# Batched matmul on one core: longer weight runs with quarter-lane casts on two engines, and a store lag that grows

## Chip, cores, metric

One NeuronCore of a Trainium2 chip. The metric is the time of one execution in microseconds on the device. Engines are named as the profile names them: PE (TensorE), DVE (VectorE), ACT (ScalarE), SP (SyncE, which here issues every DMA). Sixteen DMA engines serve the core. PSUM is the memory that PE writes its results to. A lane is one of the 128 partitions that an instruction works on at a time.

## The reference

```python
x:      (8, 16, 256, 512) float32
weight: (8, 16, 512, 384) float32
out = np.matmul(x, weight)          # 128 products of 256x512 by 512x384
```

That is 67.1 MB of x, 100.7 MB of weights and 50.3 MB of results: 218.1 MB in all.

## The kernel before

Four of the 128 products make a group, 32 groups in all. Per group the kernel loads x (2 MB, runs of 16 KB: 8 rows of a partition) and the weights (two loads of 1.5 MB, runs of 12 KB), casts both to bf16, transposes x on PE, multiplies, copies the result out of PSUM and stores it (1.5 MB, runs of 12 KB). DVE casts the weights, ACT casts x and copies results out.

```python
G = 4; C = P // G; R = G * M // P; T = R // 2      # C = 32, R = 8, T = 4
D = 2; S = 2; HP = P // D                          # two products stacked in one weight load
XS, WS, OS = 2, 2 * G // D, 4                      # x, weight and output buffers
LAG = 4                                            # stores run four groups behind loads
...
def load(e, t, U, s):                              # on SP
    e.wait_ge(x_cast, ...)                         # x buffer free: x of group n-2 is cast
    e.dma_start(x_sb[s % XS][:], ...)
    for d in range(G // D):
        e.wait_ge(w_cast, ...)                     # weight buffer free: its casts are done
        e.dma_start(w_sb[slot][:], ...rearrange("(p k) n -> p k n", k=S * KO))
...
def prepare(e, t, U, s):                           # on DVE
    for d in range(G // D):
        e.wait_ge(w_in[slot], ...)
        for a in range(D):
            for h in range(S):                     # 8 casts of 64 lanes x 1536 per group
                e.tensor_copy(out=w_bf[...][h * HP : (h + 1) * HP], in_=w_sb[slot][...])
    for q in range(T):
        e.tensor_copy(out=x_t[...], in_=pt[...])   # transposed x out of PSUM
...
def step(t, U, s, more):                           # on ACT
    for q in range(T):
        copy_out(e, t, U, s, q)
        if q == 1 and more:
            cast_x(e, t, U, s + 1)                 # x of the next group
```

All DMAs go through one queue in program order. So a load that waits for its buffer also holds back what comes after it.

Of the kernel before, what the change touches and what calls it, by code (L numbers as in the profile page):

```python
# [11 lines left out]
def kernel(  # L12
# [7 lines left out]
    P = 128  # L20

    b1, b2, M, K = x.shape
    _, _, _, N = weight.shape
    B = b1 * b2
    KO = K // P

    x_rows = x.rearrange("b1 b2 m k -> (b1 b2 m) k")
    w_rows = weight.rearrange("b1 b2 k n -> (b1 b2 k) n")
    o_rows = out.rearrange("b1 b2 m n -> (b1 b2 m) n")

    fp32 = mybir.dt.float32
    bf16 = mybir.dt.bfloat16
# [2 lines left out]




    G = 4
    C = P // G  # L40
    R = G * M // P
    T = R // 2
    D = 2
    S = 2
    HP = P // D
    NG = B // G

    XS, WS, OS = 2, 2 * G // D, 4
    BS, TS, WBS = 1, 2, 2 * G
    PT, PO = 4, 2  # L50

    LAG = 4

    ctx.enter_context(tc.tile_critical(no_gpsimd_drain=True))  # L54

    def sbuf(name, shape, dtype, n):
        return [
            ctx.enter_context(nc.sbuf_tensor(f"{name}{s}", shape, dtype)) for s in range(n)
        ]
# [6 lines left out]
    def sems(name, n):  # L66
        return [tc.alloc_semaphore(f"{name}{s}") for s in range(n)]
# [2 lines left out]
    identity = sbuf("identity", [P, P], fp32, 1)[0]  # L70
    x_sb = sbuf("x_sb", [P, R, K], fp32, XS)

    x_bf = sbuf("x_bf", [P, R, S, HP, KO], bf16, BS)
    x_t = sbuf("x_t", [P, R, KO // 2, P, 2], bf16, TS)
    w_sb = sbuf("w_sb", [P, S * KO, N], fp32, WS)
    w_bf = sbuf("w_bf", [P, KO, N], bf16, WBS)
    out_sb = sbuf("out_sb", [P, R, N], fp32, OS)
    pt = psum("pt", [P, 2, KO // 2, P], fp32, PT)
    po = psum("po", [P, 2, 512], fp32, PO)
# [1 line left out]



    id_done, x_cast, w_cast, t_made, t_copied, p_made, o_copied = (
        sems(name, 1)[0]
        for name in (
            "id_done", "x_cast", "w_cast", "t_made", "t_copied", "p_made", "o_copied"
        )
    )
    x_in, w_in, o_out = sems("x_in", XS), sems("w_in", WS), sems("o_out", OS)  # L90


    BIAS = 8


    def load(e, t, U, s):
        n = t * U + s
        if not isinstance(n, int) or n >= XS:
            e.wait_ge(x_cast, n + (1 - XS))
        e.dma_start(  # L100
            x_sb[s % XS][:],
            x_rows[bass.ds(n * (G * M), G * M)].rearrange("(p r) k -> p r k", r=R),
        ).then_inc(x_in[s % XS], 16)
        for d in range(G // D):
            slot = (s * (G // D) + d) % WS
            if not isinstance(n, int) or n >= 2:
                e.wait_ge(w_cast, n * (G * S) + ((d + 1) * D * S - 2 * G * S))
            e.dma_start(  # L108
                w_sb[slot][:],
                w_rows[bass.ds(n * (G * K) + d * (D * K), D * K)].rearrange(  # L110
                    "(p k) n -> p k n", k=S * KO
                ),
            ).then_inc(w_in[slot], 16)

    def store(e, t, U, s, pieces=1):
        n = t * U + s
        dram = o_rows[bass.ds(n * (G * M), G * M)].rearrange("(p r) n -> p r n", r=R)
        for q in range(pieces):
            rows = slice(q * R // pieces, (q + 1) * R // pieces)
            e.wait_ge(o_copied, n * T + ((q + 1) * T // pieces + BIAS))  # L120
            e.dma_start(out=dram[:, rows], in_=out_sb[s % OS][:, rows]).then_inc(
                o_out[s % OS], 16
            )

    def cast_x(e, t, U, s):
        n = t * U + s
        e.wait_ge(x_in[s % XS], (t * (U // XS) + s // XS) * 16 + 16)
        e.wait_ge(t_made, n * T + ((1 - BS) * T + BIAS))
        for h in range(S):
            ins = e.copy(  # L130
                out=x_bf[s % BS][:, :, h],
                in_=x_sb[s % XS][:].rearrange("p r (q s c) -> p r s q c", s=S, c=KO)[
                    :, :, h
                ],
            )
        ins.then_inc(x_cast, 1)

    def prepare(e, t, U, s):
        n = t * U + s
        e.wait_ge(p_made, n * T + (BIAS - T))  # L140
        for d in range(G // D):
            slot = (s * (G // D) + d) % WS
            e.wait_ge(  # L143
                w_in[slot], (t * (U * G // D // WS) + s * G // D // WS) * 16 + 16
            )
            for a in range(D):
                for h in range(S):
                    e.tensor_copy(  # L148
                        out=w_bf[(s * G + d * D + a) % WBS][h * HP : (h + 1) * HP],
                        in_=w_sb[slot][a * HP : (a + 1) * HP, h * KO : (h + 1) * KO, :],  # L150
                    ).then_inc(w_cast, 1)
        for q in range(T):
            e.wait_ge(t_made, n * T + (q + 1 + BIAS))
            e.tensor_copy(  # L154
                out=x_t[s % TS][:, 2 * q : 2 * q + 2],
                in_=pt[(s * T + q) % PT][:].bitcast(bf16),
            ).then_inc(t_copied, 1)

    def multiply(e, t, U, s):
        n = t * U + s  # L160
        words = x_bf[s % BS][:].rearrange("p r s q c -> p r (s q c)").bitcast(fp32)
        e.wait_ge(x_cast, n + 1)
        for q in range(T):
            e.wait_ge(t_copied, n * T + (q + 1 - PT + BIAS))
            for rr in range(2):
                for h in range(KO // 2):
                    ins = e.transpose(  # L167
                        pt[(s * T + q) % PT][:, rr, h, :],
                        words[:, 2 * q + rr, h :: KO // 2],
                        identity[:],  # L170
                    )
            ins.then_inc(t_made, 1)
        e.wait_ge(w_cast, n * (G * S) + G * S)
        for q in range(T):
            e.wait_ge(t_copied, n * T + (q + 1 + BIAS))
            e.wait_ge(o_copied, n * T + (q + 1 - PO + BIAS))
            for rr in range(2):
                for ko in range(KO):
                    for i in range(G):
                        mine = slice(i * C, (i + 1) * C)  # L180
                        ins = e.matmul(  # L181
                            po[(s * T + q) % PO][mine, rr, :N],
                            x_t[s % TS][:, 2 * q + rr, ko // 2, mine, ko % 2],
                            w_bf[(s * G + i) % WBS][:, ko, :],
                            start=(ko == 0),
                            stop=(ko == KO - 1),
                        )
            ins.then_inc(p_made, 1)

    def copy_out(e, t, U, s, q):  # L190
        n = t * U + s
        if q == 0:
            e.wait_ge(o_out[s % OS], (t * (U // OS) + s // OS) * 16 + 16)
        e.wait_ge(p_made, n * T + (q + 1 + BIAS))
        e.copy(  # L195
            out=out_sb[s % OS][:, 2 * q : 2 * q + 2, :],
            in_=po[(s * T + q) % PO][:, :, :N],
        ).then_inc(o_copied, 1)
# [6 lines left out]

    def on_sync(e):
        U = OS
        for n in range(LAG):
            load(e, 0, NG, n)
        rounds = (NG - LAG) // U  # L210
        with e.Fori(0, rounds) as t:
            for s in range(U):
                load(e, t, U, LAG + s)
                store(e, t, U, s)
        for n in range(rounds * U, NG):
            if n + LAG < NG:
                load(e, 0, NG, n + LAG)
            store(e, 0, NG, n, T if n == NG - 1 else 1)
        for s in range(OS):
            e.wait_ge(o_out[s], 16 + 16 * (NG // OS + (T - 1 if s == (NG - 1) % OS else 0)))  # L220

    def on_vector(e):
        U = 2
        e.sem_inc(t_copied, BIAS)
        with e.Fori(0, NG // U) as t:  # L225
            for s in range(U):
                prepare(e, t, U, s)

    def on_tensor(e):
        U = 2  # L230
# [7 lines left out]
    def on_scalar(e):  # L238
        U = OS
        e.sem_inc(o_copied, BIAS)  # L240
        for s in range(OS):
            e.sem_inc(o_out[s], 16)

        def step(t, U, s, more):
            for q in range(T):
                copy_out(e, t, U, s, q)
                if q == 1 and more:
                    cast_x(e, t, U, s + 1)

        cast_x(e, 0, NG, 0)  # L250
        with e.Fori(0, NG // U - 1) as t:
            for s in range(U):
                step(t, U, s, True)
        for n in range(NG - U, NG):
            step(0, NG, n, n < NG - 1)

    on_gpsimd(nc.gpsimd)
    on_sync(nc.sync)
    on_vector(nc.vector)
    on_tensor(nc.tensor)  # L260
    on_scalar(nc.scalar)


# [28 lines left out]
```

## Time and profile before

| | before |
|---|---|
| median (lowest to highest) | 519.68 us (519.66 to 520.01, 3 runs) |
| span of the profiled run | 518.0 us |
| DMA: bytes, mean rate | 218.1 MB, 421 GB/s |
| busy share PE, DVE, ACT | 61%, 63%, 41% |

How to read it: "share" is the part of the span in which an engine worked; the DMA row of the slices gives the busy tenths of the 16 DMA engines in each fortieth of the span. A row of nines in DMA with every compute engine near 60% says that the stream of bytes sets the time. The lines themselves stand in the prediction below.

### The profile page before, as it was taken

What the parts mean: (1) busy time and instruction counts of PE and PEld (TensorE: products, weight loads), DVE (VectorE), ACT (ScalarE), POOL (GpSimd) and SP (SyncE); (2) the same over time, 40 slices, a digit from 0 to 9 for tenths busy, and PEclk for the clock granted to TensorE, in tenths of its full rate; (3) what the DMA queues carried; (4) which work ended last, traced back from release to release, by engine and by line L of the source; (5) the groups of instructions that cost most, each with busy time, mean ns of one, the idle gap of its engine ahead of it and who ended that gap; (6) DMA issues with size and microseconds to landing.
All of it is one profiled execution on the core that took longest, in us unless ns stands there. A gap on an engine that the chain in (4) does not pass through costs nothing.

```text
span 518.0 us, 11228 instructions
## 1 busy us (share of the span) xinstructions
PE 315.0 (61%) x4608; PEld 198.0 (38%) x4608; DVE 323.9 (63%) x384; ACT 212.8 (41%) x193; POOL 0.7 (0%) x6
## 2 busy tenths in 40 slices
PE   0685775476655676555756557665566655675654
PEld 0453443343433443333434334343344333343432
DVE  0878867655577555775556765557755577555670
ACT  3073643455234552335542345423455234553242
POOL 0000000000000000000000000000000000000000
PEclk9798976888668776868786687768777787878687
DMA  8999999999999999999999999999999999999995
GB/s 337 430 424 428 426 429 427 430 428 427 430 429 426 431 425 430 428 430 432 426 427 429 430 433 425 427 430 428 432 429 427 427 430 430 430 429 424 432 428 229
DMA packets 18868, 218.16 MB, mean 421 GB/s; under 512 B 2096, under 2 KB 2096, under 8 KB 2608
## 3 DMA queue, kind: packets, MB, share of 16 engines
q1 hardware_dynamic: 18864, 218.11, 99.2%
q8 instruction: 2, 0.03, 0.0%
q14 instruction: 2, 0.02, 0.0%
HBM read 167.77 MB, written 50.33 MB: 421 GB/s over the span
## 4 chain that ended last, share of the span: by engine, by line
DMA 82%; DVE 13%; issue 2%; PE 2%; SPq 1%; ACT 0%; DVEq 0%
DMA w_sb<-in_weight_dram 82%; DVE w_bf L148 13%; PE po L181 2%; SPq L108 0%; SPq L100 0%; ACT out_sb L195 0%; DVE x_t L154 0%; DVEq L143 0%; DVEq L225 0%; SPq L287 0%; SPq L54 0%
## 5 line engine op out<-in xcount | busy, mean ns | idle before, releaser
L148 DVE CAST w_bf<-w_sb 64x1536 bf16<-64x1536 f32 x256 | 244.4, 955 | 179.4 <-DMA w_sb<-in_weight_dram 172.3
L181 PE MATMUL po<-w_bf,x_t 128*32 128x384 bf16 x4096 | 233.5, 402 | 122.2 <-DVE x_t L154 122.2
L195 ACT COPY out_sb<-po 128x768 f32<-128x768 f32 x128 | 99.4, 803 | 291.0 <-PE po L181 291.0
L181 PEld LDWEIGHTS po<-w_bf,x_t 128*32 128x32 bf16 x4096 | 125.8, 117 | 227.0 <-DVE x_t L154 131.7
L167 PE MATMUL pt<-identity,x_bf 128*128 128x128 f32 x512 | 81.5, 322 | 73.4 <-ACT x_bf L130 73.4
L130 ACT CAST x_bf<-x_sb 128x2048 bf16<-128x2048 f32 x64 | 118.5, 1902 | 6.3 <-DMA x_sb<-in_x_dram 6.3
L167 PEld LDWEIGHTS pt<-identity,x_bf 128*128 128x128 f32 x512 | 72.2, 212 | 85.2 <-issue 85.2
L154 DVE COPY x_t<-pt 128x1024 bf16<-128x1024 bf16 x128 | 79.5, 682 | 1.0
L130 ACT ACT_TABLE_LOAD x1 | 1.3, 1283 | 1.3 <-PEq L231 1.3
masks.py:199 POOL TENSOR_SCALAR_AFFINE_SELECT identity<-identity 128x128 f32<-128x128 f32 x1 | 0.3, 293 | 0.2 <-POOL identity L201 0.2
L201 POOL MEMSET identity<- 128x128 f32 x1 | 0.2, 205 | 0.5 <-SPq L54 0.5
L276 POOL MEMSET const-uint8-127<- 128x1 uint8 x1 | 0.1, 103 | 0.0
L276 POOL MEMSET const-bfloat16-1.0<- 128x1 bf16 x1 | 0.1, 102 | 0.0
L276 POOL MEMSET const-float32-0.0<- 128x1 f32 x1 | 0.1, 99 | 0.2 <-issue 0.2
L276 POOL MEMSET const-float32-1.0<- 128x1 f32 x1 | 0.1, 99 | 0.0
## 6 DMA issues: line engine op xcount, KB each, us to landing
w_sb<-in_weight_dram SPq DMA_DIRECT2D x64, 1536.0 KB, 27.6
x_sb<-in_x_dram SPq DMA_DIRECT2D x32, 2048.0 KB, 25.9
out_dram<-out_sb SPq DMA_DIRECT2D x31, 1536.0 KB, 30.5
out_dram<-out_sb SPq DMA_DIRECT2D x4, 384.0 KB, 4.1
```

The source lines that it names most:

```text
L130: ins = e.copy(out=x_bf[s % BS][:, :, h], in_=x_sb[s % XS][:].rearrange("p r (q s c) -> p r s q c", s=S, c=KO)[:, :, h],)
L148: e.tensor_copy(out=w_bf[(s * G + d * D + a) % WBS][h * HP : (h + 1) * HP], in_=w_sb[slot][a * HP : (a + 1) * HP, h * KO : (h + 1) * KO, : ...
L154: e.tensor_copy(out=x_t[s % TS][:, 2 * q : 2 * q + 2], in_=pt[(s * T + q) % PT][:].bitcast(bf16),).then_inc(t_copied, 1)
L167: ins = e.transpose(pt[(s * T + q) % PT][:, rr, h, :], words[:, 2 * q + rr, h :: KO // 2], identity[:],)
L181: ins = e.matmul(po[(s * T + q) % PO][mine, rr, :N], x_t[s % TS][:, 2 * q + rr, ko // 2, mine, ko % 2], w_bf[(s * G + i) % WBS][:, ko, :], ...
L195: e.copy(out=out_sb[s % OS][:, 2 * q : 2 * q + 2, :], in_=po[(s * T + q) % PO][:, :, :N],).then_inc(o_copied, 1)
L201: e.memset(identity[:], 0.0).then_inc(id_done, 1)
L276: nc = _bacc.Bacc("TRN2", target_bir_lowering=False, num_devices=1)
```

## The change

The intent: make the weight runs 24 KB long, so that the stream has fewer runs. A partition then holds 16 rows of weights, and the four products of a group lie in four quarters of 32 partitions. Bringing each product to all 128 partitions now takes 16 casts of 32 lanes in place of 8 of 64; three of four go to DVE, one to ACT. Because casts take longer, the stores run two groups behind the loads at first, then three, then four. The last group's weights come in two loads of 12 KB runs, cast by DVE alone in half lanes. (Cuts are marked; the comments in the diff are added here.)

```diff
-    XS, WS, OS = 2, 2 * G // D, 4
-    LAG = 4
+    XS, WS, OS = 2, 2, 4
+    V = G - 1
+    LAGS = ((2, 2), (3, 2), (4, 2))          # (lag, rounds of four groups)
...
-    w_sb = sbuf("w_sb", [P, S * KO, N], fp32, WS)
+    w_sb = sbuf("w_sb", [P, G * KO, N], fp32, WS)
...
+    def load_w(e, t, U, s):
+        if not isinstance(n, int) or n >= WS:
+            e.wait_ge(v_cast, (n - WS + 1) * (G * V))
+            e.wait_ge(a_cast, (n - WS + 1) * G)
+        e.dma_start(
+            w_sb[s % WS][:],
+            w_rows[bass.ds(n * (G * K), G * K)].rearrange("(p k) n -> p k n", k=G * KO),
+        ).then_inc(w_in[s % WS], 16)
...
+    def cast_w(e, cast, t, U, s, i, parts, done):
+        for h in parts:                       # DVE: h = 0, 1, 2; ACT: h = 3
+            cast(
+                out=w_bf[(s * G + i) % (2 * G)][h * C : (h + 1) * C],
+                in_=w_sb[s % WS][i * C : (i + 1) * C, h * KO : (h + 1) * KO, :],
+            ).then_inc(done, 1)
...
+        for lag, rounds in LAGS:              # on SP
+            while loads < stores + lag:
+                load(e, 0, NG, loads)
+                loads += 1
+            with e.Fori(0, rounds) as t:
+                for s in range(U):
+                    load(e, t, U, loads + s)
+                    store(e, t, U, stores + s)
...
+        def step(t, U, s, left=2):            # on ACT
+            if left > 1:
+                casts(t, U, s + 1, (0, 1))    # waits until the next weights have landed
+            for q in range(T):
+                copy_out(e, t, U, s, q)
+                if left:
+                    cast_x(e, t, U, s + 1, q, G if left > 1 else D)
+            if left > 1:
+                casts(t, U, s + 1, (2, 3))
```

Each time the lag grows, two loads stand in the queue with no store between them. I call that a lag step. The steps come at groups 10 to 11 and 19 to 20. Two smaller changes are not in the cuts: the x casts of a group are four of 1024 elements in place of two of 2048, and transposed x has one buffer in place of two.

More of the change, by code (lines that the diff above doesn't have):

```diff
@@ L42 @@
     T = R // 2
+    NG = B // G
+    V = G - 1
     D = 2
-    S = 2
-    HP = P // D
-    NG = B // G
-    XS, WS, OS = 2, 2 * G // D, 4
-    BS, TS, WBS = 1, 2, 2 * G
+    XS, WS, OS = 2, 2, 4
     PT, PO = 4, 2
-    LAG = 4
+    LAGS = ((2, 2), (3, 2), (4, 2))
     ctx.enter_context(tc.tile_critical(no_gpsimd_drain=True))
@@ L71 @@
     x_sb = sbuf("x_sb", [P, R, K], fp32, XS)
-    x_bf = sbuf("x_bf", [P, R, S, HP, KO], bf16, BS)
-    x_t = sbuf("x_t", [P, R, KO // 2, P, 2], bf16, TS)
-    w_sb = sbuf("w_sb", [P, S * KO, N], fp32, WS)
-    w_bf = sbuf("w_bf", [P, KO, N], bf16, WBS)
+    x_bf = sbuf("x_bf", [P, R, K], bf16, 1)[0]
+    x_t = sbuf("x_t", [P, R, KO // 2, P, 2], bf16, 1)[0]
+    w_sb = sbuf("w_sb", [P, G * KO, N], fp32, WS)
+    w_bf = sbuf("w_bf", [P, KO, N], bf16, 2 * G)
     out_sb = sbuf("out_sb", [P, R, N], fp32, OS)
@@ L79 @@
     po = psum("po", [P, 2, 512], fp32, PO)
-    id_done, x_cast, w_cast, t_made, t_copied, p_made, o_copied = (
+    id_done, x_cast, v_cast, a_cast, t_made, t_copied, p_made, o_copied = (
         sems(name, 1)[0]
         for name in (
-            "id_done", "x_cast", "w_cast", "t_made", "t_copied", "p_made", "o_copied"
+            "id_done", "x_cast", "v_cast", "a_cast",
+            "t_made", "t_copied", "p_made", "o_copied",
         )
@@ L90, with load_x @@
     x_in, w_in, o_out = sems("x_in", XS), sems("w_in", WS), sems("o_out", OS)
+    w_last = sems("w_last", D)
     BIAS = 8
-    def load(e, t, U, s):
+    def load_x(e, t, U, s):
         n = t * U + s
         if not isinstance(n, int) or n >= XS:
-            e.wait_ge(x_cast, n + (1 - XS))
+            e.wait_ge(x_cast, (n - XS + 1) * T)
         e.dma_start(
@@ L103, in load, with load_last @@
         ).then_inc(x_in[s % XS], 16)
-        for d in range(G // D):
-            slot = (s * (G // D) + d) % WS
-            if not isinstance(n, int) or n >= 2:
-                e.wait_ge(w_cast, n * (G * S) + ((d + 1) * D * S - 2 * G * S))
+    def load_w(e, t, U, s):
+        n = t * U + s
+        if not isinstance(n, int) or n >= WS:
[5 more added lines that the diff above has]
+        ).then_inc(w_in[s % WS], 16)
+    def load(e, t, U, s):
+        load_x(e, t, U, s)
+        load_w(e, t, U, s)
+    def load_last(e):
+        n = NG - 1
+        load_x(e, 0, NG, n)
+        e.wait_ge(v_cast, (n - WS + 1) * (G * V))
+        e.wait_ge(a_cast, (n - WS + 1) * G)
+        for d in range(D):
             e.dma_start(
-                w_sb[slot][:],
-                w_rows[bass.ds(n * (G * K) + d * (D * K), D * K)].rearrange(
-                    "(p k) n -> p k n", k=S * KO
+                w_sb[n % WS][:, d * D * KO : (d + 1) * D * KO],
+                w_rows[bass.ds(n * (G * K) + d * D * K, D * K)].rearrange(
+                    "(p k) n -> p k n", k=D * KO
                 ),
-            ).then_inc(w_in[slot], 16)
+            ).then_inc(w_last[d], 16)
     def store(e, t, U, s, pieces=1):
@@ L123, in store, with cast_x @@
             )
-    def cast_x(e, t, U, s):
+    def cast_x(e, t, U, s, q, S=G):
         n = t * U + s
-        e.wait_ge(x_in[s % XS], (t * (U // XS) + s // XS) * 16 + 16)
-        e.wait_ge(t_made, n * T + ((1 - BS) * T + BIAS))
-        for h in range(S):
-            ins = e.copy(
-                out=x_bf[s % BS][:, :, h],
-                in_=x_sb[s % XS][:].rearrange("p r (q s c) -> p r s q c", s=S, c=KO)[
-                    :, :, h
-                ],
-            )
-        ins.then_inc(x_cast, 1)
@@ L138, in prepare @@
-    def prepare(e, t, U, s):
+        if q == 0:
+            e.wait_ge(x_in[s % XS], (t * (U // XS) + s // XS) * 16 + 16)
+        e.wait_ge(t_made, n * T + (q + 1 - T + BIAS))
+        rows = slice(2 * q, 2 * q + 2)
+        e.copy(
+            out=x_bf[:, rows].rearrange("p r (s q c) -> p r s q c", s=S, c=KO),
+            in_=x_sb[s % XS][:, rows].rearrange(
+                "p r (q s c) -> p r s q c", s=S, c=KO
+            ),
+        ).then_inc(x_cast, 1)
+    def cast_w(e, cast, t, U, s, i, parts, done):
[4 more added lines that the diff above has]
+            ).then_inc(done, 1)
@@ L139, in prepare, with cast_w_start @@
+    def cast_w_start(e, t, U, s):
         n = t * U + s
         e.wait_ge(p_made, n * T + (BIAS - T))
-        for d in range(G // D):
-            slot = (s * (G // D) + d) % WS
-            e.wait_ge(
-                w_in[slot], (t * (U * G // D // WS) + s * G // D // WS) * 16 + 16
-            )
-            for a in range(D):
-                for h in range(S):
-                    e.tensor_copy(
-                        out=w_bf[(s * G + d * D + a) % WBS][h * HP : (h + 1) * HP],
-                        in_=w_sb[slot][a * HP : (a + 1) * HP, h * KO : (h + 1) * KO, :],
-                    ).then_inc(w_cast, 1)
+        e.wait_ge(w_in[s % WS], (t * (U // WS) + s // WS) * 16 + 16)
@@ new lines, in cast_w_last @@
+    def cast_w_last(e):
+        n = NG - 1
+        e.wait_ge(p_made, n * T + (BIAS - T))
+        H = P // D
+        for d in range(D):
+            e.wait_ge(w_last[d], 16)
+            for a in range(D):
+                for h in range(D):
+                    ins = e.tensor_copy(
+                        out=w_bf[(n * G + d * D + a) % (2 * G)][h * H : (h + 1) * H],
+                        in_=w_sb[n % WS][
+                            a * H : (a + 1) * H, (d * D + h) * KO : (d * D + h + 1) * KO, :
+                        ],
+                    )
+        ins.then_inc(v_cast, G * V)
@@ L152, in prepare, with evacuate @@
+    def evacuate(e, t, U, s):
+        n = t * U + s
         for q in range(T):
@@ L154, in prepare @@
             e.tensor_copy(
-                out=x_t[s % TS][:, 2 * q : 2 * q + 2],
+                out=x_t[:, 2 * q : 2 * q + 2],
                 in_=pt[(s * T + q) % PT][:].bitcast(bf16),
@@ L160, in multiply @@
         n = t * U + s
-        words = x_bf[s % BS][:].rearrange("p r s q c -> p r (s q c)").bitcast(fp32)
-        e.wait_ge(x_cast, n + 1)
+        words = x_bf[:].bitcast(fp32)
         for q in range(T):
+            e.wait_ge(x_cast, n * T + (q + 1))
             e.wait_ge(t_copied, n * T + (q + 1 - PT + BIAS))
@@ L172, in multiply @@
             ins.then_inc(t_made, 1)
-        e.wait_ge(w_cast, n * (G * S) + G * S)
+        e.wait_ge(v_cast, n * (G * V) + G * V)
+        e.wait_ge(a_cast, n * G + G)
         for q in range(T):
@@ L182, in multiply @@
                             po[(s * T + q) % PO][mine, rr, :N],
-                            x_t[s % TS][:, 2 * q + rr, ko // 2, mine, ko % 2],
-                            w_bf[(s * G + i) % WBS][:, ko, :],
+                            x_t[:, 2 * q + rr, ko // 2, mine, ko % 2],
+                            w_bf[(s * G + i) % (2 * G)][:, ko, :],
                             start=(ko == 0),
@@ L207, in on_sync @@
         U = OS
-        for n in range(LAG):
-            load(e, 0, NG, n)
-        rounds = (NG - LAG) // U
-        with e.Fori(0, rounds) as t:
-            for s in range(U):
-                load(e, t, U, LAG + s)
-                store(e, t, U, s)
-        for n in range(rounds * U, NG):
-            if n + LAG < NG:
-                load(e, 0, NG, n + LAG)
-            store(e, 0, NG, n, T if n == NG - 1 else 1)
+        loads = stores = 0
+        for lag, rounds in LAGS:
[6 more added lines that the diff above has]
+                    store(e, t, U, stores + s)
+            loads += rounds * U
+            stores += rounds * U
+        while stores < NG:
+            if loads < NG - 1:
+                load(e, 0, NG, loads)
+                loads += 1
+            elif loads == NG - 1:
+                load_last(e)
+                loads += 1
+            store(e, 0, NG, stores, T if stores == NG - 1 else 1)
+            stores += 1
         for s in range(OS):
@@ L224, in on_vector, with step @@
         e.sem_inc(t_copied, BIAS)
-        with e.Fori(0, NG // U) as t:
-            for s in range(U):
-                prepare(e, t, U, s)
+        def step(t, U, s):
+            cast_w_start(e, t, U, s)
+            for i in range(G):
+                cast_w(e, e.tensor_copy, t, U, s, i, range(V), v_cast)
+            evacuate(e, t, U, s)
+        with e.Fori(0, NG // U - 1) as t:
+            for s in range(U):
+                step(t, U, s)
+        for n in range(NG - U, NG - 1):
+            step(0, NG, n)
+        cast_w_last(e)
+        evacuate(e, 0, NG, NG - 1)
     def on_tensor(e):
@@ L242, in on_scalar, with casts @@
             e.sem_inc(o_out[s], 16)
-        def step(t, U, s, more):
+        def casts(t, U, s, group):
+            if group[0] == 0:
+                cast_w_start(e, t, U, s)
+            for i in group:
+                cast_w(e, e.copy, t, U, s, i, range(V, G), a_cast)
+        def step(t, U, s, left=2):
+            if left > 1:
+                casts(t, U, s + 1, (0, 1))
             for q in range(T):
                 copy_out(e, t, U, s, q)
-                if q == 1 and more:
-                    cast_x(e, t, U, s + 1)
-        cast_x(e, 0, NG, 0)
+                if left:
[3 more added lines that the diff above has]
+        for q in range(T):
+            cast_x(e, 0, NG, 0, q)
+        casts(0, NG, 0, (0, 1, 2, 3))
         with e.Fori(0, NG // U - 1) as t:
             for s in range(U):
-                step(t, U, s, True)
+                step(t, U, s)
         for n in range(NG - U, NG):
-            step(0, NG, n, n < NG - 1)
+            step(0, NG, n, min(NG - 1 - n, 2))
+            if n == NG - 3:
+                e.drain().then_inc(a_cast, G)
     on_gpsimd(nc.gpsimd)
```

## The prediction

> **What bounds the kernel now.** I read the page from the top: span, the forty slices, the DMA queues, then the costliest groups, then the waits of the DMA queue, and last the end of the run in one-microsecond windows. First the slices and the queue:
>
> ```profile
> span 518.0 us, 11228 instructions
> PE 315.0 (61%) x4608; PEld 198.0 (38%) x4608; DVE 323.9 (63%) x384; ACT 212.8 (41%) x193; POOL 0.7 (0%) x6
> ...
> DMA  8999999999999999999999999999999999999995
> GB/s 337 430 424 428 426 429 427 430 428 427 430 429 426 431 425 430 428 430 432 426 427 429 430 433 425 427 430 428 432 429 427 427 430 430 430 429 424 432 428 229
> ...
> q1 hardware_dynamic: 18864, 218.11, 99.2%
> ```
>
> No compute engine is above 63%; the 16 DMA engines are full from the second slice to the last but one, at 424 to 433 GB/s. The kernel is a stream of 218.1 MB, and the time is that stream's length plus a start and an end. Next, what each compute instruction costs, since the change moves work among them:
>
> ```profile
> L148 DVE CAST w_bf<-w_sb 64x1536 bf16<-64x1536 f32 x256 | 244.4, 955 | 179.4 <-DMA w_sb<-in_weight_dram 172.3
> ...
> L195 ACT COPY out_sb<-po 128x768 f32<-128x768 f32 x128 | 99.4, 803 | 291.0 <-PE po L181 291.0
> ...
> L130 ACT CAST x_bf<-x_sb 128x2048 bf16<-128x2048 f32 x64 | 118.5, 1902 | 6.3 <-DMA x_sb<-in_x_dram 6.3
> ```
>
> VectorE idles 172.3 us for weights to land: it starves for data, it does not hold it up. Then the waits of the DMA queue itself:
>
> ```profile
> SPq L100 <- ACT x_bf L130: 259.1, 30, 10.2
> SPq L108 <- DVE w_bf L148: 136.1, 58, 3.6
> SPq L121 <- ACT out_sb L195: 38.1, 6, 16.1
> ```
>
> They look like a bound and are not one: the issuer waits up to 10 us for a free buffer while a load takes 25 to 28 us from issue to landing, so a whole group (about 16 us) is queued ahead and the engines never run dry, as the slices say. Last the end, in windows whose last two columns are the DMA share and GB/s:
>
> ```profile
> 511.00:512.00 1.00, 0.00 (x0) 0.00 (x0) 0.00 (x0) 0.43 (x1) 0.00 (x0) 1.00 0.96 384
> 512.00:513.00 1.00, 0.00 (x0) 0.00 (x0) 0.00 (x0) 0.00 (x0) 0.00 (x0) 1.00 0.77 307
> 513.00:514.00 1.00, 0.00 (x0) 0.00 (x0) 0.00 (x0) 0.00 (x0) 0.00 (x0) 1.00 0.35 138
> 514.00:515.00 1.00, 0.00 (x0) 0.00 (x0) 0.00 (x0) 0.00 (x0) 0.00 (x0) 0.92 0.07 28
> 515.00:516.00 1.00, 0.00 (x0) 0.00 (x0) 0.00 (x0) 0.00 (x0) 0.00 (x0) 0.50 0.06 25
> ```
>
> A share of 0.06 is one engine of 16 working alone: one runs some 2.5 us behind the rest, and its last packets (118 ns apart to the end in the trace's packet records, so it never idles) set the end. The chain of waits names weight DMA for 82%, which is the same stream.
>
> The packet records also give the cost of one contiguous run. Between 100 and 400 us a 12,288 B run takes 462.3 ns on its engine (median 460) and a 16,384 B run 612.2 ns (median 611); a semaphore write takes 9 ns.
>
> **What the Trainium skill says.** (1) "DMA: Bandwidth & Descriptors", section "Where 436 GB/s comes from": 16 ports of 32 B at 850 MHz, 435.2 GB/s. The trace agrees: 427 to 430 in steady state, just under it, so at most 1.7% can be had from the rate. (2) Same page, "Why small descriptors are slow (HBM only)": a fixed cost of about 3 cycles per packet besides the bytes. The trace agrees in kind and shows more: at 27.2 GB/s per engine the medians leave 460 - 451.8 = 8.2 ns and 611 - 602.4 = 8.6 ns per run, nearly the same for both lengths, thus a cost per run and not per byte. (3) "VectorE: DVE Perf Modes", section "The TRN2 errata — SBUF-src ops pay a fixed extra latency per instruction": cutting a cast into more instructions pays that again[...]. The trace agrees for ScalarE: (1902 - 803) / (2048 - 768) = 0.86 ns per element and 143 ns fixed (one source is PSUM there, so an estimate). (4) "SBUF — State Buffer", section "Who interferes with whom": DMA does not contend with compute engines. The trace agrees: the rate is 425 to 429 GB/s whether a window has much or little VectorE work.
>
> **The change, part by part.**
>
> Runs of 24 KB. Each engine serves 8 of 128 partitions. Weights were 64 loads x 8 = 512 runs of 12 KB per engine; they become 31 x 8 = 248 of 24 KB and 2 x 8 = 16 of 12 KB. 248 runs vanish, at 8.4 to 10 ns: 2.1 to 2.5 us. 31 loads fewer save 31 semaphore writes of 9 ns per engine, 0.3 us. The stream shortens by 2.4 to 2.8 us. The straight line through the two means gives 13 ns per run and so 3.5 us, the most I believe. This lies on the path, as nothing else bounds the middle.
>
> Quarter-lane casts. With four groups' rows of weights stacked by quarters of the partitions, a cast is 32 x 1536. I take VectorE's time as unchanged at 955 ns, since elements per lane are the same. VectorE per group: 12 x 0.955 + 4 x 0.62 evacuations + gaps of 0.03 each = 14.4 us (now 8 x 0.955 + 2.5 = 10.3). ScalarE per group: four weight casts at 143 + 1536 x 0.86 = 1.46 us, four x casts of 1024 at 1.02 us, four output copies at 0.80 us = 13.2 us, with gaps 13.7 us (now 7.0). The stream takes 15.96 us per group (weight loads at 146.82 and 466.02 in the chain, 20 groups apart), 15.88 after. Both engines rise to some 90% and stay under it: hidden, with 1.5 us of slack.
>
> Buffers. The weight buffers hold two groups as before. Casts of group n end about 12 to 13.5 us after its weights land. The load of n+2 that waits for them is due at the engines only after a store (3.7 us), x of n+1 (4.9), its weights (7.3), another store and x of n+2: 24 us. Slack about 11 us, so this wait stays hidden.
>
> Store lag. While stores lag, loads run alone: 5.24 MB, 12.2 us per group, which is faster than VectorE's new 14.4. With four groups of that, the casts would fall behind and the DMA engines would dry up. Two groups at first, then one more twice, avoids this. It does not shorten today's stream: it pays for the new casts. A store two groups behind is due tightly, though: in the second group I work out its issue at 38 us against a stream that runs dry at 39.7.
>
> End. The last weights come as two 12 KB-run loads so that VectorE can do the first half while the second flies: eight casts of 955 ns, as now. But the group before has VectorE until about 14.4 us after its weights landed, some 1.4 us before the last load ends, so the last eight casts end 6.6 us after it (now 501.8 - 497.7 = 4.1). The last output copy then ends about 16.5 us after the last load, 13.7 now. The lagging engine still has four stores and a half to work through, 18.4 us, and reaches the last quarter-store at 17.5 us. So most of the 2.8 us hides, and 0 to 1.5 us shows, 0.8 taken.
>
> Sum: 519.68 - 2.5 + 0.8 = 518.0; with the chance that 24 KB runs do a little better than the medians say, I put 517.7.
>
> **Rivals.**
> First, a compute engine becomes the bound. For it: VectorE at 14.4 of 15.9 us, and ScalarE casts weights ahead of copying the previous group's output, so it now waits for a landing before it frees PSUM. Against it: the slack worked out above, and PE's 11 us per group. If a quarter-lane cast cost 1.1 us instead of 0.955, VectorE would need 16.2 us and the run would take some 530.
> Second, bubbles at the start: the tight store could open gaps of 1 to 3 us in the first eight groups, giving 519 to 521. For it: 1.7 us of slack in an estimate. Against it: the engines catch up 1.5 us per group.
> Third, a 24 KB run is cut in two below the program, or its cost is per byte. Nothing in this trace goes beyond 16 KB. Then only the semaphore writes go and the end shows: 520. Against it: 16 KB runs come as one packet record.
>
> **Range and chances.** The gain has a ceiling: at 435.2 GB/s the stream is 501.2 us, and with 3 us of start and 5 of drain, plus the 1.7 between span and time, nothing under about 511 is to be had, so over 2% faster (under 509.3) is nearly excluded. Best case 515 (3.5 us of stream and no loss at the end), likely 516.5 to 518.5, small bubbles to 520.5. A compute bound gets 3%.
>
> **What would show it.** Right: weight packets of 24,576 B at about 912 ns (903.5 + 8.5); a steady rate of 430 to 431 GB/s; full slices from the second on; VectorE near 88%, ScalarE near 80%, quarter-lane casts at 955 and 1460 ns; the last one-microsecond windows again one engine's. Wrong: slices of DMA below 9 in the middle, or VectorE never waiting for weights (a compute bound); dips in the first ten slices (the lag); packets of 12 or 16 KB for the weights; or a last copy so late that all engines idle before it.

## More of the kernel before

One more view matters later, the DMA issues: how long one load takes from issue to landing. It tells how much work is queued ahead of it.

```profile
x_sb<-in_x_dram SPq DMA_DIRECT2D x32, 2048.0 KB, 25.9
```

The last number is the median in us. The first x load, with nothing ahead of it, took 7.9 us, so some 18 us of other work stood ahead of the usual one: more than one whole group of 16 us.

## The result

The changed kernel took 524.32 us (524.16 to 524.65, 4 runs) against 519.73 us for the kernel before in the same rounds. The ratio is 1.0088, with a 95% interval of 1.0071 to 1.0106. A ratio is the mean time of one kernel's runs over that of the other's of the same rounds, so it is not quite the ratio of the medians. Executions over 1.5% slower than the fastest of the same kernel are left out of the means. The change made the kernel 0.9% slower; the prediction of 517.7 with a range of 515.0 to 520.6 missed.

The page of the changed kernel:

```profile
span 522.5 us, 11679 instructions
...
DMA  8999999999999999999999999999999999999984
GB/s 343 431 430 424 408 423 431 429 439 431 430 423 433 418 437 434 426 431 431 426 433 434 431 418 382 395 436 435 430 430 430 430 433 435 430 427 432 425 366 191
...
q1 hardware_dynamic: 14400, 218.11, 98.4%
```

The DMA row looks as full as before, and that is misleading. The rate row shows a dip to 382 and 395 in slices 25 and 26 (313 to 340 us), smaller dips at 408 and 418, and a weaker end (366 and 191 against 428 and 229). A packet that takes long counts as busy. The packets fell from 18,864 to 14,400 in this queue, as meant: 279 less on each of 16 engines, 248 runs and 31 semaphore writes.

The groups of instructions (busy us, then mean ns of one):

```profile
L160 DVE CAST w_bf<-w_sb 32x1536 bf16<-32x1536 f32 x372 | 353.8, 951 | 67.4 <-DMA w_sb<-in_weight_dram 54.8
...
L160 ACT CAST w_bf<-w_sb 32x1536 bf16<-32x1536 f32 x124 | 182.1, 1469 | 88.2 <-DMA w_sb<-in_weight_dram 85.9
...
L151 ACT CAST x_bf<-x_sb 128x1024 bf16<-128x1024 f32 x128 | 134.2, 1051 | 6.7 <-DMA x_sb<-in_x_dram 6.0
```

These are the predicted durations (955, 1460 and 1020) within 3%. A cast of 32 lanes costs what one of 64 lanes cost. But ACT idles 85.9 us for weights, which it never did before: two weight casts stand ahead of its output copies and x casts.

The DMA issues, to be held against the 25.9 us of before:

```profile
x_sb<-in_x_dram SPq DMA_DIRECT2D x32, 2048.0 KB, 14.3
```

**Where the time went.** The trace records each transfer's landings, one by one for the 16 DMA engines, and each packet's duration. For each transfer in its order I took its last landing and subtracted the time that all packets up to it need at their usual pace. That pace is 456.6, 608 and 908.5 ns for runs of 12, 16 and 24 KB, which is their median of 460, 611 and 912 ns less the 3 to 4 ns by which packets of one engine overlap. What is left is the time lost so far, on the engine that is last. Compared between the two kernels:

| | before | after | difference |
|---|---|---|---|
| packets at their usual pace, whole stream | 507.1 | 505.8 | -1.3 |
| lost up to group 6 before, group 5 after | 6.1 | 6.7 | +0.6 |
| lost at the step from lag 2 to 3 (group 11) | - | 0.25 | +0.25 |
| lost at the step from lag 3 to 4 (groups 20 and 21, store 16 with it) | - | 2.8 | +2.8 |
| lost slowly over the rest, up to the last load | 2.7 | 3.75 | +1.1 |
| from the last load's landing to the last store's | 19.1 | 20.3 | +1.1 |
| sum | | | +4.5 |

Only the differences add up (they come from unrounded figures): the first row holds the stores after the last load too, which the last row holds again. The spans differ by 4.5 us. The biggest term is one place. The windows around it in the changed kernel (the last two columns are the DMA share and GB/s):

```profile
300.00:308.00 8.00, 5.00 (x68) 3.56 (x64) 7.81 (x10) 6.78 (x7) 0.00 (x0) 0.93 0.97 397
308.00:316.00 8.00, 5.92 (x92) 3.62 (x88) 5.96 (x8) 5.87 (x6) 0.00 (x0) 0.71 1.01 434
316.00:324.00 8.00, 5.26 (x67) 3.75 (x60) 7.81 (x10) 7.01 (x8) 0.00 (x0) 0.88 0.99 356
324.00:332.00 8.00, 7.84 (x132) 4.82 (x123) 7.75 (x9) 7.93 (x9) 0.00 (x0) 0.79 1.01 435
332.00:340.00 8.00, 4.42 (x74) 2.97 (x73) 6.49 (x9) 4.60 (x5) 0.00 (x0) 1.00 1.00 375
```

The mean is 399 GB/s over 40 us. At the usual 428 that is 40 x (1 - 399/428) = 2.7 us lost. In the first row engines stand still for a moment (0.97); in the third and fifth they are busy but slow. The timeline just before it, of SP and ACT (start, duration, what; the wait before it in brackets):

```profile
293.96 2.96 ACT L160 CAST w_bf<-w_sb 32x1536 bf16<-32x1536 f32 x2 [1.92 <-DMA w_sb<-in_weight_dram]
...
297.77 1.05 ACT L151 CAST x_bf<-x_sb 128x1024 bf16<-128x1024 f32 x1
...
303.02 1.06 ACT L151 CAST x_bf<-x_sb 128x1024 bf16<-128x1024 f32 x1
...
304.27 0.34 SPq L103 DMA_DIRECT2D x_sb<-in_x_dram  x1
...
307.29 0.34 SPq L113 DMA_DIRECT2D w_sb<-in_weight_dram  x1
```

The weights of group 18 landed on the last engine at 293.9 us. Only then did ACT start its two weight casts, then copies and x casts by turns; the x buffer came free at 304.1, and SP could issue x of group 20 at 304.3, 10.3 us after that landing. The DMA engines are not abreast, though, and a buffer counts as landed when the last of them is done. At 293.9 the last engine was 3.8 us behind the median one, and the median one had only x and weights of group 19 left: 12.2 us, up to 306.1. (A store between the loads would have made it 15.8.) That was too little for 10.3 us of waiting and the time that x then takes to start moving: on the median engine x of group 20 landed 7.6 us after its issue, 4.9 of them moving, and 0.8 us later than the engine's pace. In windows of 1 us:

```profile
305.00:306.00 1.00, 0.00 (x0) 0.00 (x0) 0.97 (x2) 0.97 (x2) 0.00 (x0) 1.00 1.06 311
306.00:307.00 1.00, 0.00 (x0) 0.00 (x0) 1.00 (x3) 1.00 (x1) 0.00 (x0) 1.00 0.61 254
```

The last engine never ran dry: its x of group 20 came on pace, and all of its 2.8 us are packets that took longer than usual just after, 1.7 in the weights of group 20, 0.3 in store 16 and 0.7 in the weights of group 21.

### The profile page after: what moved, and what is told of

Read it like the earlier page. It is cut to its first block, busy times and chain, and to the rows that moved or that the text cites. A ratio compares the mean times of both kernels' runs of the same rounds, so it can differ in the third digit from the quotient of the medians.

```text
span 522.5 us, 11679 instructions
## 1 busy us (share of the span) xinstructions
PE 332.1 (64%) x4608; PEld 211.5 (40%) x4608; DVE 440.9 (84%) x508; ACT 402.7 (77%) x381; POOL 0.7 (0%) x6
## 2 busy tenths in 40 slices
DMA packets 14407, 218.18 MB, mean 418 GB/s; under 512 B 1601, under 2 KB 1601, under 8 KB 2113
## 3 DMA queue, kind: packets, MB, share of 16 engines
q1 hardware_dynamic: 14400, 218.11, 98.4%
## 4 chain that ended last, share of the span: by engine, by line
DMA 48%; ACT 16%; issue 12%; PE 12%; DVE 8%; ACTq 1%; SPq 0%; DVEq 0%
DMA w_sb<-in_weight_dram 48%; PE po L218 11%; ACT w_bf L160 8%; DVE w_bf L160 7%; ACT out_sb L232 4%; ACT x_bf L151 4%; DVE x_t L190 1%; PE pt L203 1%; ACTq L328 1%; ACTq L231 0%; SPq L113 0%; ACTq L149 0%; SPq L103 0%; ACTq L168 0%; SPq L112 0%
## 5 line engine op out<-in xcount | busy, mean ns | idle before, releaser
L160 DVE CAST w_bf<-w_sb 32x1536 bf16<-32x1536 f32 x372 | 353.8, 951 | 67.4 <-DMA w_sb<-in_weight_dram 54.8
L218 PE MATMUL po<-w_bf,x_t 128*32 128x384 bf16 x4096 | 251.9, 415 | 152.8 <-ACT out_sb L232 62.1
L160 ACT CAST w_bf<-w_sb 32x1536 bf16<-32x1536 f32 x124 | 182.1, 1469 | 88.2 <-DMA w_sb<-in_weight_dram 85.9
L218 PEld LDWEIGHTS po<-w_bf,x_t 128*32 128x32 bf16 x4096 | 143.3, 119 | 254.1 <-DVE x_t L190 95.8
L151 ACT CAST x_bf<-x_sb 128x1024 bf16<-128x1024 f32 x128 | 134.2, 1051 | 6.7 <-DMA x_sb<-in_x_dram 6.0
L232 ACT COPY out_sb<-po 128x768 f32<-128x768 f32 x128 | 102.3, 799 | 15.8 <-PE po L218 15.1
L203 PEld LDWEIGHTS pt<-identity,x_bf 128*128 128x128 f32 x512 | 68.2, 208 | 48.1 <-issue 45.4
L178 DVE CAST w_bf<-w_sb 64x1536 bf16<-64x1536 f32 x8 | 7.6, 955 | 0.1
## 6 DMA issues: line engine op xcount, KB each, us to landing
x_sb<-in_x_dram SPq DMA_DIRECT2D x32, 2048.0 KB, 14.3
```

Of the source, the lines that this page charges most:

```text
L151: e.copy(out=x_bf[:, rows].rearrange("p r (s q c) -> p r s q c", s=S, c=KO), in_=x_sb[s % XS][:, rows].rearrange("p r (q s c) -> p r s q c ...
L160: cast(out=w_bf[(s * G + i) % (2 * G)][h * C : (h + 1) * C], in_=w_sb[s % WS][i * C : (i + 1) * C, h * KO : (h + 1) * KO, :],).then_inc(do ...
L178: ins = e.tensor_copy(out=w_bf[(n * G + d * D + a) % (2 * G)][h * H : (h + 1) * H], in_=w_sb[n % WS][a * H : (a + 1) * H, (d * D + h) * KO ...
L203: ins = e.transpose(pt[(s * T + q) % PT][:, rr, h, :], words[:, 2 * q + rr, h :: KO // 2], identity[:],)
L218: ins = e.matmul(po[(s * T + q) % PO][mine, rr, :N], x_t[:, 2 * q + rr, ko // 2, mine, ko % 2], w_bf[(s * G + i) % (2 * G)][:, ko, :], sta ...
L232: e.copy(out=out_sb[s % OS][:, 2 * q : 2 * q + 2, :], in_=po[(s * T + q) % PO][:, :, :N],).then_inc(o_copied, 1)
```

## The experiments

All ran against the kernel before in the same rounds (519.5 to 519.8 us), five rounds each. A comparison with the changed kernel's 524.32 us is across rounds. The first theory, A: the long runs do help a little, and the loss comes from buffers that the slower casts free too late at a lag step. Its first rival, B: long reads are slow in themselves.

### Run length alone

```diff
-        e.dma_start(w_sb[s % WS][:], w_rows[...]).then_inc(w_in[s % WS], 16)
+        for d in range(D):
+            half = slice(d * D * KO, (d + 1) * D * KO)
+            e.dma_start(w_sb[s % WS][:, half], rows[:, half]).then_inc(w_in[s % WS], 16)
```

> The changed kernel with each weight load split into two loads of 12 KB runs; layout, casts, waits and store lag stay. Theory A (the 24 KB runs do shorten the stream, by 4.7 ns for each run saved on each engine, about 1.3 us in all, and what was lost was lost at the step of the store lag from 3 to 4 and at the end): the loss stays and the small gain goes, so 525 to 526 us, slow weight packets at the same groups 20 and 21. Rival B (long reads are slow in themselves: 24 KB packets cost 3.4 us of excess in the trace): the excess goes and the time falls to 521.5 to 523 us.

Measured: 525.6 us (524.98 to 526.64), 1.3 us over the changed kernel, as A said. The time lost up to the last load is the same (13.6 us against 13.45), and the loss at groups 20 and 21 is there with 12 KB runs too. B falls: the long runs are worth 1.3 us, and nothing of the loss is theirs.

### The lag stops at three

```diff
-    LAGS = ((2, 2), (3, 2), (4, 2))
+    LAGS = ((2, 4), (3, 3))
```

> The changed kernel with the store lag going 2 to 3 and staying there; no step from 3 to 4. Theory A: the 2.8 us that the stream loses at groups 20 to 22 go, the rest stays: 521.0 to 522.2 us. Rival B (long reads) : unchanged at 524.3. Rival C (the end is bound by the late casts of the last two groups): with one store fewer behind the last load the end gets worse, 525 to 527.

Measured: 523.67 us (522.83 to 524.61). Mostly a miss for A: only 0.65 us came back. The trace says why. The one step that was left, from 2 to 3, now stood at groups 18 and 19, and there it cost 2.6 us, where the same step at group 11 had cost 0.25. So the size of a step's loss does not come from the lag's value; it grew with time. The end changed too: with one store fewer behind the last load, all engines ran dry and waited for the last outputs.

### No step at all

```diff
-    LAGS = ((2, 2), (3, 2), (4, 2))
+    LAGS = ((2, 7),)
```

> The changed kernel with the stores two groups behind all the time. Theory A: no step at all, so the stream loses 3 us less than the changed kernel up to the last load, but only two stores are left to fill the wait for the last two groups, which costs 1 to 4 us at the end: 521 to 525 us, with a visible gap after the last load. Rival D (a lag of 2 is too tight all along, because a store is issued barely before it is due): dips in the whole middle and over 526.

Measured: 527.04 us (525.73 to 528.01), outside A's range. No loss at groups 19 to 21 (8.4 us lost in all at group 20, against 10.35 in the changed kernel), but from store 19 on the stores were not ready when due (0.9 us went at group 22's weights), and up to the last load 13.7 us were lost after all. Then the end: the median engine's store of group 30 came 7.9 us late. Rival D holds for the second half of the run.

### The kernel before with only the new lags

```diff
-    LAG = 4
+    LAGS = ((2, 2), (3, 2), (4, 2))      # and the loop of the changed kernel on SP
```

> The kernel before with only the store lag of the changed kernel (2, then 3, then 4). Theory A says that a step costs only where the casts hold the weight buffers long (13.4 us from landing to release in the changed kernel, 8 us before): 519.3 to 520.3, as before. Rival E (two loads in a row cost by themselves, whatever the casts): 2 to 3 us slower, 522 to 523.

Measured: 520.65 us (520.63 to 520.75), ratio 1.0018 (1.0004 to 1.0032). A little over A's range and far from rival E: the growing lag alone costs 0.9 us. In the trace there is no loss at group 20; the last engine loses 0.8 us at group 22, two groups after the step. Now the change is split: lags +0.9; from there to 12 KB runs with the new casts +5.0 (525.6 - 520.65); the 24 KB runs -1.3.

### Casts cut to half (a wrong result on purpose)

```diff
-                out=w_bf[...][h * C : (h + 1) * C],
-                in_=w_sb[s % WS][i * C : (i + 1) * C, h * KO : (h + 1) * KO, :],
+                out=w_bf[...][h * C : (h + 1) * C, : KO // 2],
+                in_=w_sb[s % WS][i * C : (i + 1) * C, h * KO : h * KO + KO // 2, :],
...
-                            w_bf[(s * G + i) % (2 * G)][:, ko, :],
+                            w_bf[(s * G + i) % (2 * G)][:, ko % 2, :],
```

> Wrong result on purpose: the changed kernel with every quarter-lane weight cast (all groups but the last) cut to half its elements, transfers, waits, order and store lag as they are. Theory A (the casts and their place in the queues hold the buffers too long, so that 15 of the 16 DMA engines run dry where two loads come in a row): VectorE near 9 us a group, buffers free some 3 us sooner, the loss at groups 19 to 22 shrinks from 2.8 to under 1 us: 520 to 522 us. Rival F (the transfers or the lag step by themselves, whatever the casts): 524.3, unchanged.

Measured: 518.75 us (518.52 to 519.35), better than A asked for, with DVE at 57% and ACT at 63%. Its last load landed at 496.0 us against 497.4 before: the 1.3 us of the long runs, all of it. Transfers and lags are those of the changed kernel, so the loss in the stream hangs on the time that the casts take. Rival F falls.

### The same steps, earlier

```diff
-    LAGS = ((2, 2), (3, 2), (4, 2))
+    LAGS = ((2, 1), (3, 1), (4, 4))
```

> The changed kernel with the two lag steps made earlier (after 4 and 8 stores in place of 8 and 16). Theory A2 (a step costs by how far the last DMA engine is behind the others at that time, since buffers come free on the last one's landing: 0.25 us lost at a spread of 2.5 us, 2.8 us at 3.8): both steps fall where the spread is about 2.5 us, so 521.3 to 522.5. Rival G (the step from 3 to 4 costs its 2.8 us wherever it stands): 524.3.

Measured: 521.5 us (520.89 to 522.35), as A2 said; rival G falls. Neither step shows a loss. The sum fits this: with the last engine 2.3 us behind, the median one still has 15.8 - 2.3 = 13.5 us of work at the landing (store, x and weights), and the changed kernel needed 10.3 us to the issue and 2.7 more until x moved, 13.0 in all; at 3.8 us behind it had 12.2. That the spread decides, and not something else that grows with time, is an estimate from these figures.

### ACT: copies and x casts first, all weight casts after

```diff
-            if left > 1:
-                casts(t, U, s + 1, (0, 1))
             for q in range(T):
                 copy_out(e, t, U, s, q)
                 if left:
                     cast_x(e, t, U, s + 1, q, G if left > 1 else D)
             if left > 1:
-                casts(t, U, s + 1, (2, 3))
+                casts(t, U, s + 1, (0, 1, 2, 3))
```

> The changed kernel with one thing reordered on ScalarE: output copies and x casts of a group first, then all four weight casts of the next group (before: two of the weight casts, which wait for the weights to land, stood ahead of them). Theory A3 (the x buffer comes free too late because the x casts queue behind a wait for weights, about 10.3 us after those landed): x buffers free about 5 us sooner, no dry spell at group 20, outputs ready sooner for the end: 520.5 to 522. Rival H (VectorE's twelve casts are what holds the loads): under 1 us won, 523.5 to 524.3.

> Both of the above, the new order on ScalarE and the earlier steps. Theory A3 with A2: the two remove the same loss, so no more than the better of them, 520 to 521.5. If it beats 519.7 I have missed a part of the loss.

Measured: 543.48 us (542.93 to 543.73), and 543.12 (542.5 to 543.61) with the early steps. Both miss by 20 us, because I had made a ring. Timeline of the first of them:

```profile
310.56 0.80 ACT L232 COPY out_sb<-po 128x768 f32<-128x768 f32 x1 [3.14 <-PE po L218]
...
318.18 5.95 ACT L160 CAST w_bf<-w_sb 32x1536 bf16<-32x1536 f32 x4
...
324.47 8.18 PE L218 MATMUL po<-w_bf,x_t 128*32 128x384 bf16 x128 [5.44 <-ACT w_bf L160]
...
327.26 0.80 ACT L232 COPY out_sb<-po 128x768 f32<-128x768 f32 x1 [3.14 <-PE po L218]
```

PE needs ACT's last weight cast before it can multiply; ACT's first copy needs PE's first product; and ACT has nothing left to do in between. Copy to copy takes 16.7 us, more than the 15.8 of the stream. The order in the changed kernel fills that gap with two weight casts. These runs say nothing about the x buffer.

### The last group cast like the others

```diff
-            elif loads == NG - 1:
-                load_last(e)
...
-        cast_w_last(e)
-        evacuate(e, 0, NG, NG - 1)
+        step(0, NG, NG - 1)
```

> The changed kernel with its last part undone: the last group's weights come in one load of 24 KB runs and are cast in quarter lanes on both engines like all others. Worked from the trace of the changed kernel: the last casts end 11.8 us after the last landing in place of 6.1, so the last output copy comes some 6 us later, 20 us after that landing; the last DMA engine is busy with stores until about 20 us after it anyway, so 3 to 4 us show: 527 to 528.5. Rival (the end is set by the last DMA engine alone): 524.3, unchanged.

Measured: 528.42 us (527.66 to 528.61). As expected, the last output copy starts at 521.2 us in place of 514.0. So this part of the change earns 4 us; without it the end is bound by the casts, with it by the last DMA engine, as the result section's sum shows.

### Longer lags at the start

```diff
-    LAGS = ((2, 2), (3, 2), (4, 2))
+    LAGS = ((4, 6),)                     # second run: ((3, 1), (4, 5))
```

> The changed kernel with the stores four groups behind from the start. My prediction said that the shorter lag at first is needed because loads alone come every 12.2 us a group and VectorE needs 14.4: two more groups of loads alone would then lose 2 x 2.2 us or more at the start, against one step saved later: 525 to 529. Rival A2 (a step is cheap while the DMA engines are still close together, and the start is as early as can be): 521 to 522.5.

> The changed kernel with a lag of three at first and four after four stores: one load more alone at the start, one early step. By the same working one more group of loads alone loses about 2.2 us at the start and the late step's 2.8 us go: 522.5 to 524.5. Rival A2: 521 to 522.

Measured: 525.0 us (524.15 to 525.49) and 523.16 us (522.17 to 524.29), at the low edge of the first range and within the second. Four groups of loads alone make the engines run dry at the start: by group 5 the first run has lost 9.5 us, the changed kernel 6.7. So the short lag at first is needed with these casts, as the prediction said, and worth 2.8 us at the start; the first run gets most of that back at group 20, where it has no step.

### ACT: x casts first, weight casts around the copies

What was still open is which buffer makes the late step dear: x, by ACT's order, or the weights, by DVE's twelve casts. This order frees the x buffer early and leaves ACT no gap:

```diff
+            if left:
+                for q in range(T):
+                    cast_x(e, t, U, s + 1, q, G if left > 1 else D)
             if left > 1:
                 casts(t, U, s + 1, (0, 1))
             for q in range(T):
                 copy_out(e, t, U, s, q)
-                if left:
-                    cast_x(e, t, U, s + 1, q, G if left > 1 else D)
-            if left > 1:
-                casts(t, U, s + 1, (2, 3))
+                if left > 1 and q % 2:
+                    casts(t, U, s + 1, (2 + q // 2,))
```

> The changed kernel with ScalarE's step in another order: the next group's x casts first (they need only x and a free x buffer), then two weight casts, then the output copies with the other two weight casts between them. By hand the x buffer comes free about 2 us after the weights of the group landed in place of 10, the weight buffer little earlier (VectorE's twelve casts set it). Theory A3 (the late x buffer is what runs the engines dry at the late step): the 2.8 us at groups 19 to 22 go to under 1: 521 to 522.5. Rival H (the weight buffer, so VectorE's casts): 523.5 to 524.5. If ScalarE is held in a ring with PE as in the reordering that failed, over 526.

> The same order with the two steps made early. Under A3 the early steps add little to it: 520.5 to 522. Under H it equals the early steps alone, 521.5. A version that beats the kernel before would need to be under 519.7, which I give one chance in six.

Measured: 520.17 us (520.05 to 520.44) with the late steps, ratio 1.0012 (0.9998 to 1.0026). The order alone returns 4.2 us. The same windows as above, of this run, then its DMA issues:

```profile
300.00:308.00 8.00, 5.64 (x92) 4.03 (x85) 7.72 (x10) 6.96 (x7) 0.00 (x0) 0.93 0.98 422
308.00:316.00 8.00, 5.10 (x73) 2.67 (x65) 6.22 (x7) 5.96 (x6) 0.00 (x0) 0.71 1.03 442
316.00:324.00 8.00, 5.98 (x96) 4.35 (x92) 7.78 (x11) 6.67 (x7) 0.00 (x0) 0.92 0.98 420
324.00:332.00 8.00, 4.72 (x85) 2.66 (x80) 7.75 (x9) 6.94 (x7) 0.00 (x0) 0.79 1.03 441
332.00:340.00 8.00, 5.24 (x91) 3.60 (x80) 7.81 (x10) 7.54 (x7) 0.00 (x0) 1.00 0.98 417
```

```profile
x_sb<-in_x_dram SPq DMA_DIRECT2D x32, 2048.0 KB, 22.4
```

The mean is 428 GB/s at the step that ran at 399, and an x load again has 22.4 us from issue to landing in place of 14.3. SP issued x of group 20 at 293.4 us, 11 us earlier than in the changed kernel, while the weights of group 20 went out only at 305.6 (307.3 in the changed kernel). DVE's casts are as they were, so rival H falls: it was the x buffer.

The step is not all of the 4.2 us. In the traces, whose spans differ by 4.0 us, the last engine loses 0.5 us in place of 2.8 at groups 20 and 21. Most of the other 1.7 us is the slow loss, which shrank too: over groups 6 to 19 from 1.9 us (0.25 of it the early step) to 1.3, and from group 22 to the last load from 2.1 to 1.0. Why ACT's order acts on that is not shown.

With the early steps as well: 519.25 us (518.91 to 519.41) against 519.54, ratio 0.9992 (0.9979 to 1.0006). Better than I expected, and the lowest correct one, but not to be told apart from the kernel before.

## Why the prediction was wrong

Held against its own steps:

- **What bounds the kernel: right.** The stream did, before and after. DVE and ACT stayed under their limits (84% and 77% of the span); the casts took the predicted times.
- **24 KB runs: right in sign, half in size.** Packets of 24,576 B at 912 ns came as written, and no run was cut in two. But I priced a saved run at 8.4 to 10 ns, from the packets' own durations. Packets of one engine overlap by 3 to 4 ns, so two of 12 KB for one of 24 KB saves 2 x 456.6 - 908.5 = 4.7 ns. Sum: 248 x 4.7 + 31 x 5 ns = 1.3 us in place of 2.5, and the run with 12 KB runs measured 1.3.
- **Buffers: the step that failed.** I worked out the slack of the weight buffers ("Slack about 11 us") and never that of the x buffers. ACT's new order tied the x casts to the landing of the weights; I had even written, under the first rival, that ACT "now waits for a landing before it frees PSUM", and did not follow that to the x buffer. The prediction's cover, "a whole group (about 16 us) is queued ahead", held for the kernel before and not for this one: an x load's time from issue to landing fell from 25.9 to 14.3 us, and at the late step, where no store lies between two loads, the median engine had 12.2 us queued where 13.0 were needed. It was dry for 0.8 us, and with the slow packets that followed the step cost 2.8 us. Three runs remove this loss from three sides: halved casts, earlier steps, and ACT's other order, which alone of the three changes when x is freed and leaves DVE's casts as they are.
- **Store lag: half right.** The short lag at the start is needed with these casts (2.8 us at the start without it). But I counted the later steps as free.
- **End: the 0.8 us came out as 1.1, for another reason.** I expected late output copies, the last one 16.5 us after the last load; it ended 14.0 us after it, as before. Most engines did stand still at 505 to 508 us, waiting for them (DMA share 0.26 at 506 to 507), yet the last one never waited; it came to its last stores 5.7 us behind the median, before 3.5, and took 20.3 us over them in place of 19.1. The last windows of the changed kernel show it alone for over three microseconds:

```profile
516.00:517.00 1.00, 0.00 (x0) 0.00 (x0) 0.00 (x0) 0.00 (x0) 0.00 (x0) 1.00 0.70 280
517.00:518.00 1.00, 0.00 (x0) 0.00 (x0) 0.00 (x0) 0.00 (x0) 0.00 (x0) 1.00 0.06 25
518.00:519.00 1.00, 0.00 (x0) 0.00 (x0) 0.00 (x0) 0.00 (x0) 0.00 (x0) 1.00 0.07 27
519.00:520.00 1.00, 0.00 (x0) 0.00 (x0) 0.00 (x0) 0.00 (x0) 0.00 (x0) 0.62 0.06 18
```

- **Rivals.** The second, bubbles "in the first eight groups", named the right kind of event in the wrong place: the first groups cost 0.6 us, the late step 2.8. The third, runs cut in two, did not happen, nor did the first as written.

**What stays open.** After the dry moment, some 60 packets of two weight loads took 1.0 to 2.3 us where 0.912 is usual. On the last engine they and store 16 are the whole 2.8 us, on the median engine some 2 us beside 0.8 of standstill. They stand after the dry step in the runs that had one (the changed kernel, its 12 KB form, the one whose lag stops at three, the one with the plain last group) and are missing at that place in those that had none. But most runs with the new casts show some near 50 to 65 us too, and why packets turn slow is not shown: that the dry moment brings them on is argued from where they stand. Nor is it shown why one DMA engine falls behind by some 0.2 us per group, mostly at the stores, in the later part of the run (0.09 in the kernel before), nor why less so with halved casts. The trace does not say which engine it is.

## What to carry to other kernels

When a change moves work onto an engine that also frees buffers, write down for every buffer, not only the one that changed, when it is freed and when its next load is due; an in-order engine that waits for one thing delays everything behind it. Take that slack at the tightest moment of the schedule (here where two loads follow each other without a store, with the slowest DMA engine's landing as the start), not in the steady state. The time from issue to landing of a load is the quickest gauge: its fall from 25.9 to 14.3 us warned of this while the row of DMA nines did not.

## What the Trainium skill lacked or had wrong

- "DMA: Bandwidth & Descriptors", section "Why small descriptors are slow (HBM only)", gives a fixed cost per packet in cycles, worked out for short descriptors, and no measured one for runs of 12 KB and up. Here halving the number of such runs saved 4.7 ns each, net of overlap, while the packets' own durations suggest 8.
- The same page, section "Latency and other measured facts", says that DMA engines 7 and 15 are usually slower and, as a best guess, puts that down to software-generated descriptors. Here nearly all traffic is on the hardware queue (218.11 of 218.18 MB), and one engine, which of them the trace does not say, is still 4.1 us (before) and 6.9 us (after) behind the median at the store of group 29.
- That a load is done when its slowest engine is can be gathered from the pages; that the other engines then have that much less work queued when a buffer comes free stands in none: 3.8 us less at the step that ran dry.
- No page has the slow packets that follow a dry moment: 24,576 B in 1.0 to 2.3 us against 0.912.
